# First norm of a two-block model kernel: the modulation summed on TensorE instead of VectorE

## The chip, the cores and the metric

The kernel runs on one core of a Trainium2 chip. The metric is the device time of one execution in microseconds (us). Engines are named as in the profile: PE is TensorE (PEld its weight loads), DVE is VectorE, ACT is ScalarE, POOL is GpSimd, SP is SyncE, whose queue issues the DMAs here.

## The reference, cut to what matters

The reference runs two blocks on 256 tokens of width 1024: the first has two layers with modulated norms (a gated recurrent mixer, then a product-key expert layer; a linear recurrent mixer, then the expert layer again), the second two layers of its own with convolutional feed-forward parts. All is fp32. The change touches only the first norm of the first layer, and what feeds the first product behind it:

```
cond = jax.nn.silu(c)                                   # c: (1, 1024)
mod = (cond @ w_ada[i] + b_ada[i])[:, None, :]          # w_ada[i]: (1024, 6144)
sh1, sc1, g1, sh2, sc2, g2 = jnp.split(mod, 6, axis=-1)
h = rms_norm(x, norm_g[i, 0]) * (1.0 + sc1) + sh1
proj = h @ w_in                                         # first line of the mixer; w_in: (1024, 5120)
```

For layer 0 the first norm needs sh1 and sc1: a vector of 1024 times a matrix of 1024 x 2048, 8 MB of weights that are used once.

## The kernel before

Activations lie with the feature in the partition: x is 8 tiles of 128 features by 256 tokens. Every large product is done in three fp32r products of split operands: a weight block of eight 128x128 tiles comes by DMA into a `raw` buffer (4 of them), ACT writes its rounded high part `whi` (line 283), and DVE or POOL the low part `wlo` as a difference (line 285); for each weight tile `mm3` issues hi by xh (line 415), hi by xl (416) and lo by xh (417) on PE. `Stream` hands out the tiles and prefetches blocks; split blocks have three buffers. `lo_pool` says which blocks have their low part made on POOL.

`first_norm` works on the 2048 columns of w_ada in four quarters of 512. For each quarter four pieces `ada0` of 512 KB are loaded (all sixteen have a buffer of their own, so their DMAs are issued at once, with three blocks of `hg_in` among them); a piece holds two of the eight parts k of 128 rows. DVE scales the part k=0 by the condition's column (line 681) and adds the other seven with one scaled addition each (line 683), into `acc`, 128 x 512. Four PE matmuls by a column of ones (line 686) then sum `acc` over the partitions into four columns of PSUM. Line 690 adds the bias, line 693 makes the gain, and for two of the eight feature tiles line 697 makes the normed x, ACT its high part xh (line 698), and DVE its low part xl (line 699). Ahead of the quarters stand the sums of squares of x (line 498, by ones), whose root is needed for line 697.

The first four output tiles of the product h @ w_in run over k together (`lead`), so that the products of a feature tile can start once this tile of h is there: each quarter makes two feature tiles, and these feed 2 x 4 weight tiles, 24 products, one block of weights. Behind them the main stream goes output tile by output tile.

`warm` issues products of constants (line 477) whose result is not read; `WARM_0` of them stand behind the squares and `WARM_Q` behind each quarter's sums. `behind` only fixes the order. On PE each fp32 matmul of this program is two records, a pair of load and matmul each; an fp32r one is one.

The order of instructions on each engine is made by a scheduler that simulates the program when it is built; instructions that were written earlier come first among those that it takes to be ready. PE, DVE, ACT, POOL and SP each then work through their queue in that order.

Of the kernel before, what the change touches and what calls it, by code (L numbers as in the profile page):

```python
# [12 lines left out]
F32 = mybir.dt.float32  # L13
# [4 lines left out]
OP = mybir.AluOpType  # L18
# [5 lines left out]
KD = 8  # L24
# [83 lines left out]
TOP_STEPS, POOL_LO = 64, 44  # L108
WV = 3, 2
HELD = 2  # L110
WARM_0, WARM_Q = 20, 9
OUT_LO = 3
YB_LO, BD_LO, XB_SP, BD_HI, LY, YL, YB_HI = 8, 4, 2, 9, 1, 4, (3, 4, 5)
HELD_O, DIFF = 2, 3
# [228 lines left out]
class Ker:  # L343
# [124 lines left out]
        lo = s.actp.tile([128, kt, S], F32R, name="xl", tag="xl")  # L468
        return hi, lo

    def warm(s, n, first):

        if not n:
            return
        ps = s.ac()[:, 0:128]
        for _ in range(n):
            s.behind(s.nc.tensor.matmul(ps, s.ones, s.ident, start=True, stop=True), first)


    def square_sum(s, ps, o, src, acc=None, added=ADDED):  # L480

# [175 lines left out]
    def first_norm(s):  # L657


        nc = s.nc  # L660
        hi, lo = s.acts()
        with s.tc.tile_pool(name="ada0", bufs=1) as pool:
            w_in = Stream(s, "hg_in", lo_pool=lambda b: b < 6)
            raw = []
            for q in range(4):
                for i in range(4):
                    t = pool.tile([128, 2, 512], F32, name="ada0", tag="ada0", bufs=16)
                    nc.sync.dma_start(t, s.d["ada_first"][4 * q + i].rearrange("p (a b) -> p a b", a=2))
                    raw += [t[:, 0, :], t[:, 1, :]]
                if q < 3:  # L670
                    w_in.prefetch()
            s.x_squares()
            r = pool.tile([128, S], F32, name="rstd")
            s.rstd(r, s.ssq, 0)
            s.warm(WARM_0, s.last)
            s.ahead = w_in
            gsc = pool.tile([128, KD], F32, name="gsc", tag="gsc")
            sh, sc = s.mod[0][:, 0:8], s.mod[0][:, 8:16]
            for q in range(4):
                acc = pool.tile([128, 512], F32, name="acc", tag="acc", bufs=2)  # L680
                nc.vector.tensor_scalar(acc, raw[8 * q], s.cond[:, 0:1], None, op0=OP.mult)
                for k in range(1, KD):
                    nc.vector.scalar_tensor_tensor(acc, raw[8 * q + k], s.cond[:, k:k + 1], acc, op0=OP.mult, op1=OP.add)
                ps = s.stat()
                for j in range(4):
                    last = nc.tensor.matmul(ps[:, j:j + 1], acc[:, j * 128:(j + 1) * 128], s.ones[:, 0:1],
                                            start=True, stop=True)
                s.warm(WARM_Q, last)
                two = lambda m: m[:, 0:16].rearrange("p (e j) -> p e j", e=2)[:, :, 2 * q:2 * q + 2]
                nc.vector.tensor_tensor(two(s.mod[0]), ps[:, 0:4].rearrange("p (e j) -> p e j", e=2),  # L690
                                        two(s.v("b_ada")), op=OP.add)
                sl = slice(2 * q, 2 * q + 2)
                nc.vector.scalar_tensor_tensor(gsc[:, sl], sc[:, sl], 1.0, s.v("norm_g", 2 * q, 2),
                                               op0=OP.add, op1=OP.mult)
                for k in (2 * q, 2 * q + 1):
                    t = pool.tile([128, S], F32, name="xn", tag="xn", bufs=2)
                    nc.vector.scalar_tensor_tensor(t, s.x[:, k, :], gsc[:, k:k + 1], r, op0=OP.mult, op1=OP.mult)
                    nc.scalar.activation(hi[:, k, :], t, AF.Identity, bias=sh[:, k:k + 1])
                    nc.vector.scalar_tensor_tensor(lo[:, k, :], t, sh[:, k:k + 1], hi[:, k, :].bitcast(F32),
                                                   op0=OP.add, op1=OP.subtract)  # L700
        return hi, lo
# [1133 lines left out]
```

## Time and profile before

| what | value |
|---|---|
| median of 3 runs | 3035.58 us (3031.94 to 3043.15) |
| the profiled execution's own time | 3039.8 us |
| its span, from first to last instruction | 3038.0 us |
| mean granted TensorE clock | 0.977 |
| PE, DVE, ACT, POOL busy | 94%, 74%, 49%, 14% of the span |
| DMA | 503.66 MB, 166 GB/s in the mean |

A busy PE is not PE at its peak, since matmuls are pipelined; the pace is read from the start of one record to the start of the next. The granted clock is given as a share of 2.4 GHz: 1.00, or 0.50 for 1.2 GHz. Times in the views are counted from the start of the span.

### The profile page before, as it was taken

To read this page: it belongs to the slowest core of one execution; us is meant where nothing else is said; L and a number is where in the kernel's file an instruction comes from. 1 tells how busy PE (TensorE), PEld (TensorE's weight loads), DVE (VectorE), ACT (ScalarE), POOL (GpSimd) and SP (SyncE) were. 2 spreads that over 40 slices of the span, in tenths; PEclk is the share of its full clock that TensorE was granted. 3 is DMA by queue.
4 is the path that set the end of the run, shared out by engine and by line. 5 is a ranking of instruction groups with operands and counts; after the bars stand their busy time and mean duration, and the time that the engine had idled before them with its cause. 6 is when DMAs were issued, how large, how long until landed. Compare 5 with 4: busy or idle time off the path is not lost. (4 is left out here: it accounts for less than half of the span.)

```text
span 3038.0 us, 58214 instructions
## 1 busy us (share of the span) xinstructions
PE 2868.7 (94%) x23408; PEld 2768.7 (91%) x23408; DVE 2249.4 (74%) x4115; ACT 1480.1 (49%) x2584; POOL 416.1 (14%) x260
## 2 busy tenths in 40 slices
PE   7999989999999998798999999999999989999898
PEld 7988989999999997698999999999888889977898
DVE  8997996887567659899788855555754688665885
ACT  3335434444444445554444444444744666455663
POOL 2232231000000004513200000000132020211201
PEclk9999999999999999899999999999999999999999
DMA  7655445555678763454555555665444346543454
GB/s 254 202 186 164 143 144 175 156 161 168 205 258 272 253 215 113 124 170 145 161 158 160 161 171 182 183 185 182 152 81 73 109 141 184 178 121 83 145 181 132
DMA packets 140143, 503.66 MB, mean 166 GB/s; under 512 B 15816, under 2 KB 18776, under 8 KB 139488
## 3 DMA queue, kind: packets, MB, share of 16 engines
q1 hardware_dynamic: 139872, 499.93, 53.7%
q8 instruction: 184, 3.01, 0.4%
q14 instruction: 87, 0.71, 0.1%
HBM read 496.72 MB, written 1.05 MB: 164 GB/s over the span
## 5 line engine op out<-in xcount | busy, mean ns | idle before, releaser
L415 PE MATMUL psmm<-xh,whi 128*128 128x256 f32 x5488 | 1568.2, 288 | 45.0 <-ACT xh L463 18.3
L417 PE MATMUL psmm<-xh,wlo 128*128 128x256 f32 x5488 | 1560.5, 286 | 40.4 <-DVE wlo L285 36.2
L416 PE MATMUL psmm<-xl,whi 128*128 128x256 f32 x5488 | 1565.7, 286 | 5.3 <-DVE xl L554 2.8
L283 ACT CAST whi<-raw 128x1024 fp32r<-128x1024 f32 x819 | 857.5, 1048 | 1231.6 <-PE psmm L416 924.7
L285 DVE TENSOR_TENSOR wlo<-raw,whi 128x1024 fp32r<-128x1024 f32 x740 | 939.7, 1272 | 452.0 <-ACT whi L283 445.7
L415 PEld LDWEIGHTS psmm<-xh,whi 128*128 128x128 f32 x5488 | 1058.6, 194 | 57.8 <-ACT xh L463 19.8
L417 PEld LDWEIGHTS psmm<-xh,wlo 128*128 128x128 f32 x5488 | 1062.2, 194 | 46.9 <-DVE wlo L285 41.8
L416 PEld LDWEIGHTS psmm<-xl,whi 128*128 128x128 f32 x5488 | 1065.0, 194 | 9.6 <-DVE xl L554 4.8
L285 POOL TENSOR_TENSOR wlo<-raw,whi 128x1024 fp32r<-128x1024 f32 x90 | 229.3, 2552 | 492.9 <-ACT whi L283 429.7
L285 POOL TENSOR_TENSOR Ar<-raw,Ar 128x1024 fp32r<-128x1024 f32 x4 | 9.6, 2402 | 1310.4 <-ACT Ar L283 1310.4
L415 PE MATMUL psst<-xh,whi 128*128 128x256 f32 x400 | 119.8, 301 | 0.0
L416 PE MATMUL psst<-xl,whi 128*128 128x256 f32 x400 | 118.9, 298 | 0.3 <-DVE xl L645 0.3
L417 PE MATMUL psst<-xh,wlo 128*128 128x256 f32 x400 | 118.0, 296 | 0.7 <-DVE wlo L285 0.7
L415 PE MATMUL psmm<-yh,whi 128*128 128x256 f32 x352 | 98.2, 280 | 0.0
L417 PE MATMUL psmm<-yh,wlo 128*128 128x256 f32 x352 | 97.9, 278 | 0.0
L416 PE MATMUL psmm<-yl,whi 128*128 128x256 f32 x352 | 97.5, 277 | 0.0
L713 DVE SCALAR_TENSOR_TENSOR oh<-raw,cond,oh 128x1024 f32<-128x1024 f32 x42 | 53.9, 1284 | 55.8 <-DMA raw<-in_ada 55.8
L1198 DVE TENSOR_TENSOR oh<-io,sel 128x512 f16<-128x512 f16 x128 | 54.2, 424 | 52.8 <-PE psac L1210 26.9
L464 DVE TENSOR_TENSOR xl<-A,xh 128x512 fp32r<-128x512 f32 x128 | 87.1, 684 | 0.0
L416 PEld LDWEIGHTS psst<-xl,whi 128*128 128x128 f32 x400 | 79.1, 198 | 7.2 <-issue 5.2
L415 PEld LDWEIGHTS psst<-xh,whi 128*128 128x128 f32 x400 | 79.0, 198 | 5.5 <-issue 4.5
L417 PEld LDWEIGHTS psst<-xh,wlo 128*128 128x128 f32 x400 | 79.2, 198 | 4.3 <-issue 2.8
(576 smaller groups left out, 3924.2 us busy)
## 6 DMA issues: line engine op xcount, KB each, us to landing
raw<-in_U SPq DMA_DIRECT2D x256, 512.0 KB, 3.6
raw<-in_V SPq DMA_DIRECT2D x256, 512.0 KB, 3.7
raw<-in_up SPq DMA_DIRECT2D x88, 512.0 KB, 3.7
raw<-in_ada SPq DMA_DIRECT2D x80, 512.0 KB, 4.4
raw<-in_down SPq DMA_DIRECT2D x44, 512.0 KB, 3.7
raw<-in_ev_in SPq DMA_DIRECT2D x42, 512.0 KB, 3.6
raw<-in_hg_in SPq DMA_DIRECT2D x40, 512.0 KB, 3.7
raw<-in_peer_q SPq DMA_DIRECT2D x32, 512.0 KB, 3.9
```

The source lines that it names most:

```text
L283: keep(nc.scalar.copy(hi, raw))
L285: keep(eng.tensor_tensor(lo, raw, hi.bitcast(F32), op=OP.subtract))
L415: first = t.matmul(ps, w[0], x[0], start=start, stop=False, **kw)
L416: t.matmul(ps, w[0], x[1], start=False, stop=False, **kw)
L417: t.matmul(ps, w[1], x[0], start=False, stop=stop, **kw)
L464: s.nc.vector.tensor_tensor(lo, src, hi.bitcast(F32), op=OP.subtract)
L713: nc.vector.scalar_tensor_tensor(acc, raw, s.cond[:, k:k + 1], acc, op0=OP.mult, op1=OP.add)
L1198: nc.vector.tensor_tensor(o1l, io4, k1, op=OP.is_equal)
```

## The change

The sum over all 1024 rows is done on PE: each 128x128 part of a piece of w_ada is loaded as the stationary operand, the condition's column of 128 values is the moving one, and the eight parts k accumulate in PSUM, four columns per quarter. The scalings and additions on DVE, the products by a column of ones and all warming products go. Of the blocks of `hg_in`, POOL made the low parts 0 to 5; after the change it makes 2, 5 and 8, and DVE the others.

```
-WARM_0, WARM_Q = 20, 9
...
-            w_in = Stream(s, "hg_in", lo_pool=lambda b: b < 6)
+            w_in = Stream(s, "hg_in", lo_pool=lambda b: b % 3 == 2 and b < 9)
...
-            s.warm(WARM_0, s.last)
...
             for q in range(4):
-                acc = pool.tile([128, 512], F32, name="acc", tag="acc", bufs=2)
-                nc.vector.tensor_scalar(acc, raw[8 * q], s.cond[:, 0:1], None, op0=OP.mult)
-                for k in range(1, KD):
-                    nc.vector.scalar_tensor_tensor(acc, raw[8 * q + k], s.cond[:, k:k + 1], acc, op0=OP.mult, op1=OP.add)
+
                 ps = s.stat()
-                for j in range(4):
-                    last = nc.tensor.matmul(ps[:, j:j + 1], acc[:, j * 128:(j + 1) * 128], s.ones[:, 0:1],
-                                            start=True, stop=True)
-                s.warm(WARM_Q, last)
+                for k in range(KD):
+                    for j in range(4):
+                        nc.tensor.matmul(ps[:, j:j + 1], raw[8 * q + k][:, j * 128:(j + 1) * 128], s.cond[:, k:k + 1],
+                                         start=k == 0 and j == 0, stop=k == KD - 1, skip_group_check=True)
```

The function `warm` itself goes too.

## Rows read from the trace of the kernel before

**Rows 1.** The page's busy time, share of the span and instructions of PE.

```profile
PE 2868.7 (94%) x23408; PEld 2768.7 (91%) x23408; DVE 2249.4 (74%) x4115; ACT 1480.1 (49%) x2584; POOL 416.1 (14%) x260
```

**Rows 2.** Busy time by stretch: us, PE, PEld, DVE, ACT, POOL, clock, DMA, GB/s.

```profile
40.00:45.00 5.00, 3.38 (x24) 2.97 (x24) 4.96 (x6) 3.72 (x5) 3.17 (x2) 1.00 0.00 0
...
55.00:60.00 5.00, 4.61 (x38) 4.61 (x39) 4.19 (x15) 3.44 (x7) 0.00 (x0) 1.00 0.51 159
```

**Rows 3.** PE in order of time, 0 to 56 us: start, length, line, operation, idle before.

```profile
7.29 6.54 PE L498 MATMUL psst<-sq,cst 128*128 128x256 f32 x16 [7.29 <-DMA cst<-in_cst]
13.67 4.63 PE L477 MATMUL psac<-cst 128*128 128x128 f32 x40
...
50.57 0.74 PE L415 MATMUL psmm<-xh,whi 128*128 128x256 f32 x4 [2.10 <-ACT xh L698]
...
53.34 0.28 PE L416 MATMUL psmm<-xl,whi 128*128 128x256 f32 x1
53.46 0.28 PE L417 MATMUL psmm<-xh,wlo 128*128 128x256 f32 x1
55.39 0.39 PE L415 MATMUL psmm<-xh,whi 128*128 128x256 f32 x1 [1.66 <-ACT FF L899]
```

**Rows 4.** PE's groups by form, 0 to 56 us: busy, mean ns, idle before.

```profile
L477 PE MATMUL psac<-cst 128*128 128x128 f32 x112 | 13.6, 278 | 0.0
...
L686 PE MATMUL psst<-cst,acc 128*128 128x1 f32 x32 | 3.9, 245 | 1.7 <-DVE acc L683 1.7
```

**Rows 5.** DVE's groups by form, 0 to 56 us.

```profile
L683 DVE SCALAR_TENSOR_TENSOR acc<-ada,cond,acc 128x512 f32<-128x512 f32 x28 | 22.9, 821 | 0.5
```

**Rows 6.** DVE in order of time, 0 to 56 us.

```profile
8.55 0.49 DVE L681 TENSOR_SCALAR acc<-ada,cond 128x512 f32<-128x512 f32 x1 [7.61 <-DMA ada<-in_ada_first]
...
41.64 3.54 DVE L683 SCALAR_TENSOR_TENSOR acc<-ada,cond,acc 128x512 f32<-128x512 f32 x2
...
47.44 2.93 DVE L697 SCALAR_TENSOR_TENSOR xn<-xres,gsc,rstd 128x256 f32<-128x256 f32 x2
```

**Rows 7.** POOL's groups by form, 0 to 56 us.

```profile
L285 POOL TENSOR_TENSOR wlo<-raw,whi 128x1024 fp32r<-128x1024 f32 x6 | 15.8, 2644 | 33.5 <-ACT whi L283 33.5
```

**Rows 8.** PE's weight loads in order of time, around 18 us.

```profile
18.02 0.97 PEld L686 LDWEIGHTS psst<-cst,acc 128*128 128x128 f32 x8
18.91 0.42 PEld L477 LDWEIGHTS psac<-cst 128*128 128x128 f32 x3
```

**Rows 9.** PE's weight loads in order of time, around 2166 us.

```profile
2165.32 0.98 PEld L1369 LDWEIGHTS psac<-wab,xres 128*128 128x128 f32 x4
2166.17 0.33 PEld L416 LDWEIGHTS psmm<-xl,whi 128*128 128x128 f32 x1
2166.39 0.33 PEld L417 LDWEIGHTS psmm<-xh,wlo 128*128 128x128 f32 x1
```

**Rows 10.** Busy time by stretch around 2165 us; columns as in rows 2.

```profile
2161.80:2165.10 3.30, 1.91 (x14) 1.73 (x15) 3.30 (x12) 3.00 (x8) 0.00 (x0) 1.00 0.69 189
2165.20:2171.90 6.70, 6.70 (x33) 6.70 (x33) 6.38 (x17) 5.51 (x13) 0.20 (x2) 0.50 0.05 14
```

**Rows 11.** PE by stretch, 241 to 257 us: us, busy, clock, DMA, GB/s.

```profile
241.20:243.40 2.20, 0.00 (x0) 1.00 0.25 101
243.50:250.50 7.00, 7.00 (x16) 0.50 0.00 0
250.60:253.70 3.10, 3.10 (x16) 0.50 0.00 0
253.80:257.00 3.20, 3.20 (x29) 1.00 0.00 0
```

**Rows 12.** Busy time by stretch around 2730 us; columns as in rows 2.

```profile
2727.60:2731.70 4.10, 2.90 (x45) 2.20 (x45) 2.88 (x5) 3.01 (x8) 1.60 (x2) 1.00 0.41 124
2731.80:2737.70 5.90, 3.95 (x17) 2.14 (x13) 4.28 (x21) 2.87 (x11) 0.00 (x0) 0.50 0.33 83
```

**Rows 13.** PE in order of time, around 245 us (rows * columns of the array).

```profile
243.43 7.17 PE L772 MATMUL psmm<-hrstd,cst 8*128 8x256 f32 x16 [2.33 <-DVE hrstd L768]
```

More of the change, by code (lines that the diff above doesn't have):

```diff
@@ L469, in acts @@
         return hi, lo
[L471 to L477, printed above, removed]
     def square_sum(s, ps, o, src, acc=None, added=ADDED):
```

## The prediction

> **What bounds the kernel now.** I read the page first, then the engines' time by stretch for the first 60 us, then each engine's order of time there. Over the whole span TensorE is busy 94% of the time [rows 1]; the reader should see that a stretch in which TensorE does something else than the big products is paid almost in full. The change lies in such a stretch, the first 55 us. There VectorE is the bound: it is busy 4.96 of 5 us at 40 to 45 us, while TensorE has 3.38 and the DMA share is 0.00, so every piece of w_ada has landed by then [rows 2]. TensorE's own order of time shows the sums of squares ending at 13.7 us, then products that only warm; the last quarter's real products start at 50.57 after a 2.10 us wait for the scalar engine's xh, and the last one ends at 53.46 + 0.28 = 53.74. After a wait of 1.66 us the main stream runs from 55.39 [rows 3], and at 55 to 60 us TensorE is full (4.61 of 5) [rows 2]. So the stage ends when VectorE has summed the last quarter (41.64 + 3.54 = 45.18 us) and the short chain behind it is through [rows 6]. What the change is worth is how far it moves 53.74: all behind it is the same TensorE-bound stream and moves along.
>
> **What is removed.** 28 scaled additions, 22.9 us of VectorE [rows 5], and the four scalings ahead of them, the first beginning at 8.55 us when the first piece lands [rows 6]. These were the bound of the stage. The 112 warming matmul records, 13.6 us busy [rows 4], stood while TensorE had nothing else to do; as work they free nothing that is on the path. Three of the six low parts leave GpSimd, 3 x 2.64 = 7.9 us [rows 7], and become three subtractions on VectorE, which has the room in the 22.9 us that it gives up. Where GpSimd ran at the same time, the normed x took 2.93 us for two instructions [rows 6]; a gain of about 2 us there is possible, but it counts only if VectorE's chain still ends the stage. The low part that moves the other way, block 8, lies in the main stream: 2.64 us on GpSimd in place of a VectorE subtraction, and it is prefetched three blocks ahead, that is behind two blocks of products (48 matmuls of 0.12 us, 5.8 us). I cost it at nothing; uncovered it would be at most its 2.64 us. No DMA is added or moved. The issues of w_in on SyncE wait for raw buffers as before, and the masks behind them wait for the stage's end, so they shift with it.
>
> **What is added, and its price.** Each quarter becomes 8 x 4 = 32 matmuls, 128 in all. The trace shows the same form of matmul: fp32, a stationary 128x128 and one moving column. The 16 of these in the code are 32 records [rows 4], so the change has 256 pairs of a weight load and a matmul where there were 32. With one column the load sets the pace: eight of these loads take 18.91 - 18.02 = 0.89 us, 0.111 us each, at the full clock of 2.4 GHz [rows 8]. At half clock (1.2 GHz) the nearest rows are the fp32 loads before 12 moving columns: (2166.17 - 2165.32) / 4 = 0.2125 us [rows 9], in a stretch with a granted clock of 0.50 [rows 10]. So all the sums cost 256 x 0.111 = 28.4 us at full clock and 256 x 0.2125 = 54.4 us at half. A piece of 512 KB (16 pairs) takes 1.8 or 3.4 us; VectorE, whose 32 instructions filled the time from 8.55 to 45.18 us [rows 6], keeps only the short chains, so TensorE is the stage's bound either way.
>
> **Which clock.** This decides the case, and the rows speak for the half. Before 2165 us TensorE did eight such thin matmuls, a few wide ones and some waiting (busy 1.91 of 3.30 us); the clock then fell to 0.50 and stayed there for 6.7 us of 100% busy time [rows 10]. A wait of 2.2 us came before the fall at 243.5, and then 7.00 of 7.00 us of busy time, 16 records that stream only 8 of the 128 rows, ran at 0.50 to their end [rows 11, 13]; the clock came back after 3.1 us of wide products [rows 11]. And at 2727.6 to 2731.7 TensorE was busy 2.90 of 4.10 us with 45 records, nearly all small; then it fell, and stayed at 0.50 for the next 5.90 us [rows 12]. In these rows records that keep little of the array moving don't hold the clock, however close together they stand. A stream of one moving column is the thinnest that there can be, and the wide warming products that stood between the sums are gone. The Trainium skill says otherwise: in "TensorE: Matmul & The Clock Gate", section "Why this matters for your kernels", throughput drops come from idle gaps between bursts of matmuls, and sums without gaps would keep the full clock, which gives the first rival's time. The 7.00 busy us at 0.50 disagree with that reading [rows 11]. Its section "LDWEIGHTS (loading the stationary operand)" has a load's time depend on the columns alone, 128 / 1.2 = 107 ns by its formula, so by an estimate from that page the sums would be 256 x 0.107 = 27.4 us at either clock. The rows have 0.111 us at full and 0.2125 us at half, and the measurement decides.
>
> **The sum.** The squares end at 13.7 us as before, with the clock full for the warming products that followed [rows 3]. Behind them stand 256 pairs and the 72 products of the first three quarters (8 weight tiles of three products each per quarter). A wide product takes 0.12 us at full clock (53.46 - 53.34) [rows 3] and 0.22 us at half (2166.39 - 2166.17) [rows 9]. All at half clock: 54.4 + 72 x 0.22 = 15.8, together 70.2 us. Four spells of wide work (the squares, three quarters' products) can each leave a stretch of full clock behind them. The rows show such stretches of 2.2 us [rows 11] and 4.1 us [rows 12]; I take 3.2 us, in which 29 pairs are done that would take 6.1 us at half, so each gives 2.9 us back, four of them 11.7 us. The third quarter's products can be done while the last quarter's chain (modulation, normed x, xh, xl) runs, so I cost that chain at nothing; if they have been used up before, it costs about 2 us. The last 24 products take 2.9 us at full and 5.3 us at half, 4.1 us in the middle. End: 13.7 + 70.2 - 11.7 + 4.1 = 76.3 us against 53.74, that is +22.6 us. Against the profiled execution's own 3039.8 us this makes 3062.4; that execution lies 4.2 us over the median of the runs, 3035.58, to which the forecast is made: 3035.58 + 22.6 = 3058.2.
>
> Bounds: with no full clock at all and the chain uncovered, 13.7 + 70.2 + 5.3 + 2 = 91.2, +37.5 us. With the full clock throughout, 13.7 + 28.4 + 72 x 0.12 = 8.6 + 2.9 = 53.6, which is +-0 us; sums that begin between the squares, since pieces land from 8.55 us on, could take something off; I allow 3 us, half of the squares' 6.54 us [rows 3]. I am nearer to the upper end, as no row shows thin work at full clock for more than a few microseconds.
>
> **Rivals.** First, the clock holds: the end comes at about 53.6 us or up to 3 us sooner, and the time is 3033 to 3038, no change. This is the one on the other side. It is decided at one place, the sums of the first quarter after the squares: if the granted clock there is 1.00 to the end of the second quarter's sums, it holds. For it speaks that weight loads fill TensorE without a gap; against it the stretches above. Second, the order on TensorE is kinder than I take it: the scheduler places each quarter's 24 products as an unbroken burst among the sums, long enough for the clock to rise within it (3.1 us of wide products did that [rows 11]), and full clock covers half of the sums and products. Half of the 70.2 us at full clock saves some 17 us in place of 11.7, and mixed stretches hold it longer: +5 to +15 us, 3041 to 3050. For it speaks that the kernel before has its products in one or two bursts per quarter; against it that sums come first in the program and, with their data landed, are ready sooner. Third, the opposite: products are mixed so finely between sums that nothing raises the clock until the last quarter: +34 us or more, over 3070.
>
> **How the numbers follow.** The forecast, half clock for most of the sums (+16 to +34 us, 3051 to 3070), has 0.72. The clock holds: 0.12. A kinder order: 0.12. Never a rise: 0.04. The time is that of the first, 3058. The range leaves out the clock holding and the worst order, 0.16 together, and so goes from 3041, the low end of the kinder order, to 3070. The forecast's own range is 3051 to 3070. About 0.5%, 15 us, is what a measurement of this kernel can tell from no change (the three runs lie 11.2 us apart). Slower by that: nearly all of 0.72, the 0.04 and a little of the kinder order, 0.76. Within: 0.23. Faster by it: 0.01, since even the holding clock gains 3 us at most.
>
> **What would show it.** In the profile after, the first 75 us: TensorE busy from about 8 us almost without idle time; the load group of the sums with 256 records, one lasting near 0.33 us, as at half clock [rows 9]; granted clock 0.50 in most of 20 to 70 us; VectorE nearly idle until the last quarter; the main stream beginning at 74 to 88 us instead of 55.39, and everything behind it shifted by the same amount. Wrong would be: clock 1.00 through the sums (then no change); an idle TensorE that waits for pieces (then DMA bounds it, and the price of the loads is not the point); or a difference that arises behind the stage, in a changed order of the later stages, which I take to be none.

## The result and the profile after

The changed kernel took 3068.52 us in the median of 6 runs (3065.82 to 3072.62), the kernel before 3037.43 beside it (3031.94 to 3047.07): a ratio of 1.0093 [1.008, 1.0106], or 24 to 32 us more. The profiled execution took 3067.04 us against 3039.8, that is +27.2, and its span grew from 3038.0 to 3065.3 us.

The page's busy time, beside [rows 1]:

```profile
PE 2912.6 (95%) x23520; PEld 2816.3 (92%) x23520; DVE 2228.2 (73%) x4086; ACT 1481.1 (48%) x2584; POOL 408.1 (13%) x257
```

112 more records on PE (256 - 32 - 112) make it 43.9 us busier. DVE and POOL give up 21.2 and 8.0 us, and neither comes back as time.

PE in order of time, 0 to 84 us, where [rows 3] had the squares, the warming products and the last quarter's 24 products:

```profile
6.91 2.04 PE L489 MATMUL psst<-sq,cst 128*128 128x256 f32 x4 [6.91 <-DMA cst<-in_cst]
8.75 3.41 PE L674 MATMUL psst<-cond,ada 128*128 128x1 f32 x16
12.02 2.05 PE L489 MATMUL psst<-sq,cst 128*128 128x256 f32 x4
...
24.82 1.20 PE L489 MATMUL psst<-sq,cst 128*128 128x256 f32 x2
25.81 42.66 PE L674 MATMUL psst<-cond,ada 128*128 128x1 f32 x200
68.34 0.56 PE L414 MATMUL psmm<-xh,whi 128*128 128x256 f32 x1
68.69 0.41 PE L415 MATMUL psmm<-xl,whi 128*128 128x256 f32 x1
68.91 0.41 PE L416 MATMUL psmm<-xh,wlo 128*128 128x256 f32 x1
...
72.91 0.28 PE L414 MATMUL psmm<-xh,whi 128*128 128x256 f32 x1
73.03 0.28 PE L415 MATMUL psmm<-xl,whi 128*128 128x256 f32 x1
...
81.78 0.28 PE L416 MATMUL psmm<-xh,wlo 128*128 128x256 f32 x1
81.95 0.39 PE L414 MATMUL psmm<-xh,whi 128*128 128x256 f32 x1
```

Four things are to be seen. The sums begin between the squares, at 8.75 us, and the last two squares come at 24.82. From 25.81 on, 200 records of the sums stand in one run: 200 x 0.213 = 42.6 us. None of the products of xh and xl stands among them; all 96 (four quarters of 24) come behind, from 68.34 to 82.06. And the main stream begins at 81.95 in place of 55.39, without the wait for FF that preceded it before.

PE's weight loads by form, 0 to 82 us (busy us, mean ns, idle before):

```profile
L674 PEld LDWEIGHTS psst<-cond,ada 128*128 128x128 f32 x256 | 56.1, 333 | 1.1
L489 PEld LDWEIGHTS psst<-sq,cst 128*128 128x128 f32 x16 | 4.6, 331 | 7.2 <-ACT sq L477 6.9
```

One load lasts 0.333 us, as the loads at half clock did [rows 9]. The stretch adds up: 16 squares at 0.427 (twice 0.2133) and 256 sums at 0.2133 make 6.83 + 54.6 = 61.4 us, and 68.34 - 6.91 = 61.43. (The first four squares and 16 sums alone: 1.71 + 3.41 = 5.12 us, and 12.02 - 6.91 = 5.11.)

Busy time by stretch, columns as in [rows 2]:

```profile
40.00:45.00 5.00, 5.00 (x25) 5.00 (x25) 2.09 (x6) 0.91 (x2) 0.00 (x0) 1.00 0.00 0
60.00:65.00 5.00, 5.00 (x25) 5.00 (x25) 0.00 (x0) 0.00 (x0) 0.00 (x0) 1.00 0.00 0
73.00:78.00 5.00, 5.00 (x44) 5.00 (x43) 4.52 (x24) 2.16 (x3) 0.00 (x0) 1.00 0.49 170
```

PE is full and, at 60 to 65 us, everything else stands still: DVE, ACT and POOL have nothing to do and the DMA queues move nothing. The clock column has to be read with care here. This trace holds no record of the clock before its rise at 72.8 us, and for want of one the column shows 1.00. The pace tells the clock: at 68.69 a wide product takes 0.22 us to the next, at 72.91 it takes 0.12, which are the two paces of [rows 3] and [rows 9]. So PE ran at 1.2 GHz from the start to 72.8 us.

DVE's short chains now wait for PE. Two of them, in order of time:

```profile
54.86 0.16 DVE L677 TENSOR_TENSOR mod<-psst,vecs 128x4 f32<-128x4 f32 x1 [11.31 <-PE psst L674]
68.51 0.16 DVE L677 TENSOR_TENSOR mod<-psst,vecs 128x4 f32<-128x4 f32 x1 [11.31 <-PE psst L674]
```

A quarter's modulation comes 13.65 us after the one before it: 64 x 0.2133.

Behind the stage, the same DMA issues of the two traces lie 25 to 34 us apart along the kernel (26.6 at 133 us, 32 near 1000, 27.2 at the end). The stage makes the difference; what is added or lost later is a few us either way.

### The profile page after: what moved, and what is told of

Read it like the earlier page. It is cut to its first block, busy times and chain, and to the rows that moved or that the text cites. A ratio compares the mean times of both kernels' runs of the same rounds, so it can differ in the third digit from the quotient of the medians.

```text
span 3065.3 us, 58399 instructions
## 1 busy us (share of the span) xinstructions
PE 2912.6 (95%) x23520; PEld 2816.3 (92%) x23520; DVE 2228.2 (73%) x4086; ACT 1481.1 (48%) x2584; POOL 408.1 (13%) x257
## 5 line engine op out<-in xcount | busy, mean ns | idle before, releaser
L284 POOL TENSOR_TENSOR wlo<-raw,whi 128x1024 fp32r<-128x1024 f32 x87 | 222.8, 2564 | 533.7 <-ACT whi L282 479.1
```

Of the source, the lines that this page charges most:

```text
L284: keep(eng.tensor_tensor(lo, raw, hi.bitcast(F32), op=OP.subtract))
```

## The experiments

The theory: the sums cost 256 x 0.213 us since such thin records leave PE at half clock, and PE is what ends the stage. Its rivals: the loads are that slow by themselves or by their data, whatever the clock; the warming products or the low parts, which go with the change, make the difference; the order does, since all products stand behind all sums. "Last product" is the end of the 96 products before the main stream: 53.74 us before, 82.06 after. Ratios are to the kernel before on the same chip.

**The warming products alone** (in the kernel before):

```
-WARM_0, WARM_Q = 20, 9
+WARM_0, WARM_Q = 0, 0
```

> The kernel before without its 56 warming matmuls (112 records), nothing else changed. Clock theory (the loss of the change is the price of the thin sums at half clock): VectorE still sets the stage's end, some products run at 0.213 us instead of 0.12, the last product ends 1 to 5 us after 53.74, and the time is within 0.3% of before. Rival (taking the warming away is what costs): the last product ends 15 us or more later, and the time rises by 0.5% or more.

Measured: 3036.85 us, ratio 0.9995 [0.9985, 1.0006]. PE in order of time, and one stretch:

```profile
49.40 1.23 PE L415 MATMUL psmm<-xh,whi 128*128 128x256 f32 x4 [1.38 <-ACT xh L698]
51.70 0.58 PE L416 MATMUL psmm<-xl,whi 128*128 128x256 f32 x1 [1.08 <-DVE xl L699]
...
55.93 0.35 PE L417 MATMUL psmm<-xh,wlo 128*128 128x256 f32 x1
```

```profile
39.20:56.00 16.80, 12.78 (x56) 12.19 (x57) 11.33 (x24) 8.25 (x14) 7.64 (x3) 0.50 0.36 120
```

The last product ends at 56.28, 2.5 us later. The clock is at 0.50 there, but PE still waits for DVE and ACT, so until the last quarter half clock costs nothing. The last 24 products begin 1.2 us sooner than before (49.40 against 50.57), then wait 1.08 us for DVE's xl, and half clock adds 24 x (0.22 - 0.12) = 2.4 us to them.

**The low parts alone** (in the kernel before):

```
-            w_in = Stream(s, "hg_in", lo_pool=lambda b: b < 6)
+            w_in = Stream(s, "hg_in", lo_pool=lambda b: b % 3 == 2 and b < 9)
```

> The kernel before with only the choice of GpSimd's low parts changed (blocks 2, 5, 8 instead of 0 to 5). Clock theory: this part is not the loss. VectorE gets four subtractions of 1.22 us on the path and loses up to 4 us of interference from GpSimd; the last product ends within 4 us of 53.74, the time is within 0.3% of before. Rival (the low parts carry a good share of the loss): 8 us or more later.

Measured: 3039.08 us, ratio 1.0002 [0.9988, 1.0015]. The last product, in PE's order of time, ends at 51.78 us, 2.0 sooner:

```profile
51.50 0.28 PE L417 MATMUL psmm<-xh,wlo 128*128 128x256 f32 x1
```

If the two add up, they make +0.5 us of the stage; in the time neither shows. What is left, some 28 us, comes with the sums. Both were tried in the kernel before only; what wide products whose results are not read do among the sums, the fourth experiment shows.

**The sums behind the squares** (in the changed kernel; `behind` fixes the order):

```
-                        nc.tensor.matmul(ps[:, j:j + 1], ...)
+                        s.behind(nc.tensor.matmul(ps[:, j:j + 1], ...), s.last)
```

> The changed kernel with all sums ordered behind the squares, so that the squares run together at the start and can raise the clock to full before the first sum. Clock theory (thin sums neither raise nor hold the clock): the sums start at 0.111 us a pair and fall to 0.213 after 2 to 5 us, though TensorE never waits; they end near 65 us instead of 68.3, and the time is 2 to 6 us under the changed kernel's. Rival (the clock was only never raised, because the squares were spread out; once up, sums without gaps hold it): 0.111 us throughout, sums end near 42 us, the last product near 54, and the time is that of before, 26 us or more under the changed kernel's.

Measured: 3068.47 us, ratio 1.009 [1.0066, 1.0114]. Here the trace records the clock from its rise at 11.6 us on, and it is the run in which the clock itself can be watched. PE in order of time:

```profile
7.38 6.57 PE L489 MATMUL psst<-sq,cst 128*128 128x256 f32 x16 [7.38 <-DMA cst<-in_cst]
...
13.79 48.46 PE L674 MATMUL psst<-cond,ada 128*128 128x1 f32 x247
...
64.03 0.56 PE L414 MATMUL psmm<-xh,whi 128*128 128x256 f32 x1
...
77.95 0.28 PE L416 MATMUL psmm<-xh,wlo 128*128 128x256 f32 x1
```

and busy time by stretch:

```profile
14.00:18.00 4.00, 4.00 (x38) 4.00 (x37) 1.23 (x1) 1.40 (x2) 0.00 (x0) 1.00 1.03 410
19.00:23.00 4.00, 4.00 (x20) 4.00 (x20) 1.85 (x2) 1.04 (x1) 0.00 (x0) 0.50 1.03 411
60.00:64.00 4.00, 4.00 (x20) 4.00 (x21) 0.00 (x0) 0.00 (x0) 0.00 (x0) 0.50 0.00 0
```

The squares raised the clock. The sums then ran at 38 pairs in 4 us, and 4.6 us into them the clock fell to 0.50 while PE had no idle time at all, and the pace went to 20 pairs in 4 us. The DMA moved 410 GB/s in both stretches, so the data is not what changed; at 60 us it moved nothing and the pace was the same 20. The Trainium skill ("TensorE: Matmul & The Clock Gate", section "Why this matters for your kernels") puts such drops down to idle gaps between bursts of matmuls; this fall came without a gap. No row of the kernel before shows such a fall: in [rows 11] the clock falls after a wait, and what follows without a gap is a clock that stays low.

**The sums filled with wide products** (the last kernel, and after every four sums one product of constants with 416 columns; 32 of these are added, and their result is not read):

```
+                    f = s.ac()[:, 0:416]
+                    s.behind(nc.tensor.matmul(f, s.ones, s.cst, start=True, stop=True), last)
```

> As the run with the squares first, with one wide product of constants (128 x 416 moving, two records, 0.69 us at full clock) behind every four sums, 32 in all, whose results are not read. Clock theory: the fill holds the clock, pairs of the sums stay at 0.111 us, and 28.4 + 32 x 0.69 = 50.6 us for sums and fill: they end near 65 us, no later than without the fill although 64 records more are done, and the products behind them start at full clock; time 2 to 8 us under the changed kernel's. Rival (a pair costs 0.213 us here for another reason than the clock, as the data or the loads): 54.5 + 22 us or more, the sums end after 90 us, and the time is 20 us or more above the changed kernel's.

Measured: 3066.03 us, ratio 1.0087 [1.0065, 1.0109]. The clock, once the squares have raised it, stands at 1.00 through sums, fill and products. PE in order of time:

```profile
44.92 0.94 PE L677 MATMUL psac<-cst 128*128 128x416 f32 x2
45.71 0.95 PE L674 MATMUL psst<-cond,ada 128*128 128x1 f32 x8
46.52 0.94 PE L677 MATMUL psac<-cst 128*128 128x416 f32 x2
...
61.51 0.36 PE L414 MATMUL psmm<-xh,whi 128*128 128x256 f32 x1
...
75.73 0.28 PE L416 MATMUL psmm<-xh,wlo 128*128 128x256 f32 x1
```

and the loads of the sums, 13 to 62 us:

```profile
L674 PEld LDWEIGHTS psst<-cond,ada 128*128 128x128 f32 x256 | 33.1, 192 | 9.0 <-issue 8.9
```

The same 256 loads last 0.192 us in place of 0.333, and eight pairs take 46.52 - 45.71 = 0.81 us, 0.101 each. So a load is not slow by itself: the clock is the cause. It can't be bought back this way, though. With 64 more records, sums and fill take 48.1 us (13.46 to 61.51) where the sums alone took 50.2 (13.79 to 64.03): 2 us won.

**The sums twice** (in the changed kernel; the second set goes to columns that nothing reads; a single run):

```
+                        nc.tensor.matmul(ps[:, 8 + j:9 + j], raw[8 * q + k][:, j * 128:(j + 1) * 128], s.cond[:, k:k + 1],
+                                         start=False, stop=k == KD - 1, skip_group_check=True)
```

> The changed kernel with every sum issued twice, the second time into columns that are not read. Clock theory with TensorE as the bound: 256 more pairs at 0.213 us, +54.6 us on the stage. Rival (pairs cost 0.111 us and the rest of the loss is order and waits): +28.4 us or less.

Measured: 3125.62 us. PE in order of time, the first product and the main stream:

```profile
122.94 0.56 PE L414 MATMUL psmm<-xh,whi 128*128 128x256 f32 x1
...
136.19 0.39 PE L414 MATMUL psmm<-xh,whi 128*128 128x256 f32 x1
```

The first product moves from 68.34 to 122.94: 54.6 us for 256 more pairs, 0.2133 each. That is the price of the disputed step by itself: PE is busy without a gap from 20 to 120 us of this run.

**The products between the sums** (in the changed kernel; each quarter's 24 products are issued behind the next quarter's sums, into the same four banks that `lead` would take):

```
+                if q:
+                    products(q - 1)
+            products(3)
```

> The changed kernel with the first products issued inside the first norm, those of a quarter directly behind the next quarter's sums, instead of all behind the last sum. Clock theory: the sums cost the same, except in the few microseconds of full clock that each burst of 24 products leaves behind it; the last product ends 2 to 9 us before the changed kernel's 82.1. Rival (the loss is that nothing overlaps, as all products stand behind all sums): it ends 20 us or more earlier, and the time is within 0.3% of before.

Measured: 3065.85 us, ratio 1.0087 [1.0072, 1.0101]. The last product ends at 79.82, 2.2 us sooner than after. PE in order of time (the last two quarters' sums and the last product), and busy time by stretch:

```profile
45.65 11.27 PE L683 MATMUL psst<-cond,ada 128*128 128x1 f32 x64
...
61.99 10.60 PE L683 MATMUL psst<-cond,ada 128*128 128x1 f32 x64
...
79.54 0.28 PE L416 MATMUL psmm<-xh,wlo 128*128 128x256 f32 x1
```

```profile
44.90:48.10 3.20, 3.20 (x31) 3.20 (x30) 1.22 (x1) 1.04 (x1) 0.00 (x0) 1.00 0.00 0
48.40:60.00 11.60, 11.60 (x55) 11.60 (x56) 2.09 (x6) 0.91 (x2) 0.00 (x0) 0.50 0.13 47
```

24 products do raise the clock. It is up from 44.8 to 48.3 us; the sums begin at 45.65 and so have it for 2.6 us, then it falls again. The order was worth 2 us of the 28.

**The operands exchanged** (in the changed kernel). The thin operand is held and the wide one moves: each part of the condition, repeated in 32 columns, is the stationary operand, and the four 128-column parts of a piece move past it into the four 32-row strips of PSUM. The result comes as rows and is turned by one ACT copy and one PE transpose per quarter:

```
+            cond = pool.tile([128, KD, 32], F32, name="cond32")
+            for k in range(KD):
+                nc.vector.tensor_scalar(cond[:, k, :], s.ones[:, 0:32], s.cond[:, k:k + 1], None, op0=OP.mult)
...
-                        nc.tensor.matmul(ps[:, j:j + 1], raw[8 * q + k][:, j * 128:(j + 1) * 128], s.cond[:, k:k + 1],
...
+                        nc.tensor.matmul(ps[32 * j:32 * j + 32, 0:128], cond[:, k, :], raw[8 * q + k][:, j * 128:(j + 1) * 128],
...
+                nc.scalar.copy(row, ps[:, 0:128])
+                nc.tensor.transpose(pt[:, 0:128], row, s.ident)
```

> The changed kernel with the operands exchanged: the condition's column, repeated in 32 columns, is the stationary operand and the pieces move, 128 columns to each of the four column tiles; a copy and a transpose turn the row into columns. Clock theory: 256 records of 128 moving columns are no thin work, so the clock rises and holds; at 0.107 us a record one after the other the sums take 27 us and the last product ends near 50 us; if the four column tiles work side by side, as the pairs of such matmuls in the later modulations do, the sums keep pace with the DMAs, whose last piece lands near 31.5 us, and the last product ends near 40 us: time 5 to 14 us under before. Rival (sums on TensorE cost the loss whichever way they are fed, since its own work is the bound): the last product ends after 65 us, and the time is 10 us or more above before.

Measured: 3033.65 us, ratio 0.9981 [0.9972, 0.9991]: faster than the kernel before by 3 to 9 us. PE in order of time:

```profile
16.77 2.23 PE L677 MATMUL psst<-ada,cond 128*32 128x128 f32 x64
...
22.30 0.64 PE L677 MATMUL psst<-ada,cond 128*32 128x128 f32 x16 [2.59 <-DMA ada<-in_ada_first]
...
24.86 1.08 PE L677 MATMUL psst<-ada,cond 128*32 128x128 f32 x16 [0.20 <-DMA ada<-in_ada_first]
25.87 1.22 PE L414 MATMUL psmm<-xh,whi 128*128 128x256 f32 x4
...
41.88 0.74 PE L414 MATMUL psmm<-xh,whi 128*128 128x256 f32 x4 [1.47 <-ACT xh L692]
...
44.18 0.58 PE L415 MATMUL psmm<-xl,whi 128*128 128x256 f32 x1 [1.57 <-DVE xl L693]
...
47.84 0.28 PE L416 MATMUL psmm<-xh,wlo 128*128 128x256 f32 x1
48.41 0.39 PE L414 MATMUL psmm<-xh,whi 128*128 128x256 f32 x1 [0.28 <-ACT FF L893]
```

There are 256 records again. At a granted clock of 1.00, 64 of them take 2.23 us, 0.035 us each, where a pair took 0.101 at 1.00 in the fourth experiment; at 0.50 the 16 at 24.86 take 1.01 us up to the next record at 25.87, 0.063 each in place of 0.213. PE now waits for the pieces: 2.59 us before a piece at 22.30, in a stretch in which the DMA brings 409 GB/s and then 411:

```profile
19.10:23.00 3.90, 0.97 (x17) 0.51 (x17) 2.61 (x4) 1.27 (x2) 0.00 (x0) 1.00 1.03 409
23.30:30.00 6.70, 6.22 (x56) 5.08 (x60) 3.74 (x9) 2.86 (x5) 1.48 (x1) 0.50 1.04 411
```

The main stream begins at 48.41, 7.0 us sooner than before and 33.5 sooner than after. The last product ends at 48.12 (47.84 + 0.28); the end near 40 us that was expected was missed. After these waits the clock stood at 0.50 from 23.3 to 30 us, and DVE's xl of the last quarter took 2.67 us for two instructions while GpSimd made a low part from 41.49 to 43.85:

```profile
41.86 2.67 DVE L693 SCALAR_TENSOR_TENSOR xl<-xn,mod,xh 128x256 fp32r<-128x256 f32 x2 [0.98 <-ACT xh L692]
```

**The same with its sums behind the squares:** as in the third experiment, `behind(..., s.last)` on line 677's products.

> As the run with the condition held, with the sums ordered behind the squares. Clock theory: if spreading the squares leaves the clock low in the first 20 us, this raises it sooner and ends the stage 0 to 4 us earlier than without the order; if the moving pieces raise it by themselves, nothing changes or the later start costs up to 3 us. Rival as for that run.

Measured: 3035.31 us, ratio 0.9986 [0.9976, 0.9996]; the main stream at 48.78, no gain. The clock rose early, at 10.4 us, but fell again from 20.6 to 30.9, where PE waits for pieces.

**The same with GpSimd's low parts later:**

```
-            w_in = Stream(s, "hg_in", lo_pool=lambda b: b % 3 == 2 and b < 9)
+            w_in = Stream(s, "hg_in", lo_pool=lambda b: b > 5 and b < 9)
```

> The run with the condition held, with GpSimd's low parts only for blocks 6 to 8, so that GpSimd doesn't run beside the last quarter's chain on VectorE (there two low parts xl took 2.67 us instead of 0.89), and with the order on TensorE that the scheduler makes of it. The last product should end 1 to 6 us before that run's 48.12; the time 0.1 to 0.4% under before. Rival: the chain's waits come from elsewhere (the turn of the row, the copy), and nothing is gained against that run.

Measured: 3035.78 us, ratio 0.9994 [0.9984, 1.0005], no change against the kernel before. The last product ends at 45.89, 2.2 us sooner. DVE's xl of the last quarter now takes 0.88 us, and PE no longer waits for it; but PE's order has changed too (its first product comes at 32.33 in place of 25.87), so the 2.2 us are not shown to be GpSimd's alone. The main stream gains only 0.9. DVE's xl, and PE in order of time:

```profile
42.31 0.88 DVE L693 SCALAR_TENSOR_TENSOR xl<-xn,mod,xh 128x256 fp32r<-128x256 f32 x2
```

```profile
45.61 0.28 PE L416 MATMUL psmm<-xh,wlo 128*128 128x256 f32 x1
47.51 0.39 PE L414 MATMUL psmm<-xh,whi 128*128 128x256 f32 x1 [1.62 <-ACT FF L893]
```

It waits for FF again, on ACT, as the kernel before did [rows 3]. The time does not show the gain: what the later stages add or lose is of that size. For the same reason the stages of the third, fourth and sixth experiment, 2 to 6 us shorter than after, don't stand out in the times; what these three say of the cause rests on their traces.

## Why the prediction was right, and where its sum was off

**Right: the bound, the clock and the price.** The stage was DVE's and became PE's, its end moved, and all behind it moved along. The sums ran at half clock throughout: 256 x 0.2133 = 54.6 us where 54.4 was predicted from [rows 9]. Filling and doubling them show both halves of that: 0.101 us a pair where the clock stays up, 54.6 us for another 256 where it does not. The first rival, a clock that holds, fell at the place that the prediction named, the first quarter's sums: in the third experiment, in which the clock was up when they began, it lasted 4.6 us.

**Right, but read from rows that do not show it: that thin records don't hold the clock.** In all three places that the prediction reads, the fall comes after waits: PE was busy 1.91 of 3.30 us before 2165 [rows 10], had waited 2.33 us before 243.43 [rows 13] and was busy 2.90 of 4.10 us before 2731 [rows 12]. And the 6.70 busy us at 0.50 after 2165 are mostly wide products: of their 33 records [rows 10] only 8 are thin. PE, PEld, clock, DMA and GB/s of that stretch, for the thin products of line 1369 alone:

```profile
2165.20:2171.90 6.70, 1.73 (x8) 2.12 (x9) 0.50 0.05 14
```

What these rows show is a clock that has fallen after waits and stays low under busy work, wide work too. That thin work without a gap brings it down was a guess from them; the third experiment shows it.

**Right by offsetting errors: the end of the stage.** By the terms of the sum, end of the last product:

| term | predicted, us | measured, us |
|---|---|---|
| squares | 13.7 (end) | 6.91 + 6.83 = 13.74 |
| 256 sums at half clock | 54.4 | 54.6 |
| full clock given back | -11.7 | 0 |
| 96 products | 15.8 + 4.1 | 13.7 |
| end | 76.3 | 82.06 |

The mis-sized term is the 11.7 us of full clock that four spells of wide work were to give back: nothing raised the clock before the sums ended. The squares, which did so before, were spread among the sums (the last two at 24.82 us, 0.427 each), and the products, which could have, all stood behind. The prediction read the same fact from the program, that sums come first in it and have their data, and used it only against the kinder order; it is what took the give-back away. The other side paid half of it: 96 products in one run raised the clock after 20 of them (68.34 to 72.8), and the other 76 took 0.12 us, so that all cost 13.7 us instead of 19.9. The squares' term came out by accident: 16 records at half clock add up to what they had taken before. So the end is 5.8 us late by the sum, +28.3 instead of +22.6. That is half of the third rival: no rise until the last sum, though by products that stood behind, not finely between.

**Off by a little: the wait behind.** The 1.66 us that the main stream waited for FF [rows 3] were not in the sum. ACT's table load for it now ends at 81.5, before the last product, and the main stream moves by 81.95 - 55.39 = 26.6 us only, the span by 27.3. The medians differ by 31.1; the interval of 24 to 32 us holds both.

**Right: what was costed at nothing.** In the kernel before, the warming products and the low parts change the stage by +2.5 and -2.0 us, and the time by nothing that shows. Four low parts leave GpSimd, not three (blocks 0, 1, 3 and 4), and block 8 comes: 8.0 us less in all, close to the 7.9 of the prediction. The chain of the last quarter stayed hidden as a wait: the sums end and the products of earlier quarters begin at once, at 68.34.

**Open:** the kinder order had 0.12. With the products between the sums, the two stretches of full clock are 3.5 and 3.4 us long, close to the 3.2 that was taken, yet the end gains only 2.2 us: the last two quarters' sums take 11.1 and 10.5 us in place of 13.65, but the products now cost 17.2 us in place of 13.7, since most of the 24 ahead of each stretch run at half clock themselves. Whether larger bursts would cover half of the stage was not tried.

## What to carry to other kernels

In a product with a single column on one side, ask which operand is held: loading 128x128 weights for one moving column cost 0.101 us a pair at full clock and 0.213 at the half clock that these sums ran at, and holding the thin operand in 32 columns while the wide one moves cost 0.035 and 0.063 a record, for the same data in as many records. Work given to the engine that bounds the kernel has to be cheaper than the wait that it removes, priced at the clock that it will itself bring about: 22.9 us less on an engine that had nothing else to do bought 54.6 us on TensorE. And where a sum counts on one kind of work lifting the clock for another, check in the program's order that it stands ahead of it.

## What was not expected of the hardware

- Forecast, but seen in no row before: TensorE's clock fell to 0.50 in a stretch without any idle time, 4.6 us of fp32 pairs with one moving column, back to back, after squares that had raised it. 64 records of 416 columns among 256 such pairs held it at 1.00.
- The time of a weight load follows the clock: 0.192 us each at 1.00, 0.333 at 0.50, and a pair with one column 0.101 to 0.105 (4.00 / 38) against 0.213 us.
- Four column strips of 32 let 64 fp32 records of 128 columns run in 2.23 us, 0.035 us each, at a granted clock of 1.00; the warming records of the same 128 columns over the full width took 13.6 / 112 = 0.121 us each [rows 4], at 1.00 too.
- A view's clock can be 1.00 for want of a record: in the trace of the changed kernel the first one is at 72.8 us, and only the pace shows 1.2 GHz before it.
